# Three paced lanes for a delta rule: one layer of a hybrid encoder on one Trainium2 core

## The chip, the core and the metric

The kernel runs on one core of a Trainium2 chip. The metric is the device time of one execution in microseconds. The engines named below are PE (TensorE: matrix multiply; PEld are its weight loads), DVE (VectorE), ACT (ScalarE), POOL (GpSimd) and SP (SyncE, which here issues all DMAs). Each engine takes its instructions in order, and instructions on different engines wait for each other through semaphores.

## The reference

One layer runs over 512 tokens of a prompt and 8 x 16 tokens of running streams, 640 tokens in all, in float32:

```python
z = x @ w_in          # q, k, v, forget, gate of branch A; q|k|v, decay, beta, gate of branch B; two merge gates
# branch A: attention with forget gates, 8 heads of 128
y_a = (o_a * silu(gate_a)) @ w_out_fox
# branch B: gated delta rule, 8 heads of 128
conv = silu(sum(xpad[:, i:i + n_tok] * gdn_conv_w[i] for i in range(4)))
q_b, k_b = l2_normalize(q_b) * GDN_SCALE, l2_normalize(k_b)
u, w = solve(amat, v * beta), solve(amat, k * beta * exp(gc))   # triangular, per chunk
v_new = u_n - w_n @ s                                          # chunk after chunk
o = q_n @ s + qk_n @ v_new
s = s * gl_n + kt_n.T @ v_new
y_b = (rms_norm(o_b) * silu(gate_b)) @ w_out_gdn
h = (sigmoid(m_a) * y_a + sigmoid(m_b) * y_b) @ w_out
x1 = layer_norm(ALPHA * x + h)
x_out = x1 + sigmoid(x1 @ w_pl_gate) * rms_norm(p @ w_pl_proj)
```

It also returns keys, values, the last rows before the convolution and the final state matrices.

## The kernel before

Every large product is computed with the features on the partitions and the 640 tokens along the free axis, cut into two halves of 320. One **column** is 128 output features: 16 k-steps, each of six matmuls of 320 tokens (`mm6`, lines 216 to 221), because each float32 operand is split into a high and a low part in a faster format (high x high, high x low, low x high). The weights come in halves of a column by DMA (`w_dma`, line 155); `w_piece` (lines 160 to 173) makes pieces of four k-steps out of them: ACT casts the high part (line 169), DVE subtracts it for the low part (line 170). `PIECES` such pieces may be ahead of PE.

The work that is not a column runs in **lanes**. A lane is a queue of Python generators that emit instructions and then yield. After each k-step `column` calls `tick`, and each lane whose wake time has come emits its next step; `yield n` means "not again before n ticks". So the order in which instructions stand in each engine's queue is fixed by hand, in ticks, when the program is built. `until(cond)` ticks without emitting columns until a condition holds; `par` runs several generators within one lane.

The program has three phases.

1. `phase_fox`: the columns of branch A with attention as side work, the first `FRONT` merge-gate columns (`mcol`), and at its end two columns for the per-layer embedding, whose sum of squares is gathered in `eacc`, a tile that is kept until the tail.
2. `phase_gdn`: for each of eight heads the columns q, k, v and gate, then `FILL` = 1 merge-gate column (after the last head six). That makes 80 ticks per head. Side work per head:
   - `conv_silu` (lines 593 to 619), lane `conv`: four taps of 664 elements on DVE (lines 601 and 605), tanh on ACT (line 610), and two DVE operations that write k, q or v.
   - `gdn` (from line 621), lane `work`: transposes and norms, the triangular matrices `lt` and `qk`, then the solve of the 32 x 32 diagonal blocks: `lt` goes to DRAM and comes back in another layout (`lanes`), 31 steps of two DVE operations (lines 727 and 729) follow, two in each tick, and the result goes through DRAM to `u0`.
   - `gdn_chunks`, lane `chunks`: `gdn_pro` builds the inverse of the blocks (line 843 transposes `u0` into `m0` on DVE, line 852 is the first matmul that reads it) and runs the four chunks of the prompt (state update at line 909); `gdn_dec` does the streams.
   - `gdn_out`, lane `ends`: normalisation, gate, and the store of the head's output. The gate tile `sg` stays on the chip from its column until then (two buffers).

   Waits in the Python loop keep buffers safe: `bdone >= h - 2` before a head's k/q tile, `gdone >= h - 2` before its gate tile, and an empty convolution lane after each column. After the eighth head's six merge-gate columns two more follow, in which the 16 head outputs are loaded back; the last of these loads waits for `gdone == 7`.
3. `tail`: output projections, merge, layer norm and the embedding gate. It reads `eacc` in `rstd`, and begins with the loads of the merge gates (line 1219); the first use is line 1239.

All phases hold their tiles in pools that follow each other in the same memory.

Of the kernel before, what the change touches and what calls it, by code (L numbers as in the profile page):

```python
# [9 lines left out]
F32 = mybir.dt.float32  # L10
# [35 lines left out]

class Kernel:
# [5 lines left out]
    PIECES = 6  # L53
    FRONT = 32 - 11 - 7
    FILL = 1
    LATE = 3

    def __init__(self, tc, ins, outs):
        self.tc, self.nc, self.i, self.o = tc, tc.nc, ins, outs
        self.lanes = []  # L60
        self.now = 0


    def lane(self):
        q = {"gens": deque(), "wake": 0}
        self.lanes.append(q)
        return q

    def tick(self):
        self.now += 1  # L70
        for q in self.lanes:
            if q["gens"] and q["wake"] <= self.now:
                self.step(q)

    def step(self, q):
        while q["gens"]:
            try:
                n = next(q["gens"][0])
                q["wake"] = self.now + (n or 1)
                return  # L80
            except StopIteration:
                q["gens"].popleft()

    def until(self, cond):

        while not cond():
            self.tick()

    def par(self, *gens):

        live = [[g, 0] for g in gens]
        t = 0
        while live:
            for e in list(live):
                if e[1] <= t:
                    try:
                        e[1] = t + (next(e[0]) or 1)
                    except StopIteration:
                        live.remove(e)
            if live:  # L100
                yield 1
                t += 1
# [490 lines left out]
    def conv_silu(self, strip, ct, dst):  # L593
# [7 lines left out]
        nc.vector.tensor_scalar(out=y[:, 0:CV], in0=strip[:, 0:CV], scalar1=tp[:, 4 * ct:4 * ct + 1], scalar2=None,  # L601
                                op0=ALU.mult)
        yield
        for i in range(1, 4):
            nc.vector.scalar_tensor_tensor(out=y[:, 0:CV], in0=strip[:, i:i + CV],  # L605
                                           scalar=tp[:, 4 * ct + i:4 * ct + i + 1], in1=y[:, 0:CV],
                                           op0=ALU.mult, op1=ALU.add)
            yield
        th = self.zt([P, SW], "cth")
        nc.scalar.activation(th[:, 0:CV], y[:, 0:CV], AF.Tanh)  # L610
        yield 2
        nc.vector.scalar_tensor_tensor(out=dst[:, 0:NPT], in0=th[:, 0:NPT], scalar=1.0, in1=y[:, 0:NPT],
                                       op0=ALU.add, op1=ALU.mult)

        def dv(x):
            return x[:, NPT + 3:SW].rearrange("p (b r) -> p b r", r=19)[:, :, 0:16]
        nc.vector.scalar_tensor_tensor(out=dst[:, NPT:T].rearrange("p (b r) -> p b r", r=16), in0=dv(th), scalar=1.0,
                                       in1=dv(y), op0=ALU.add, op1=ALU.mult)
        yield

    def gdn(self, h, kq, v, sg):
# [48 lines left out]
        cs = self.zt([P, 5, 5], "cs", 2)  # L670
# [20 lines left out]
        lt = self.zt([P, 5, P], "lt")  # L691
        qk = self.zt([P, 5, P], "qk", 2)
        for t0 in (0, 2, 4):
# [16 lines left out]
            yield (4 if t0 < 4 else 1)  # L710

        for a in range(4):
            sl = slice(32 * a, 32 * a + 32)
            nc.sync.dma_start(out=self.ld[:, a].rearrange("t j i -> j t i"), in_=lt[sl, :, sl])
        nc.vector.tensor_tensor(out=gr, in0=gr, in1=kq[:, 1, :], op=ALU.mult)
        qg = gr
        yield 5
        lanes = self.zt([80, 32, 32], "hl", 1, "lanes")
# [21 lines left out]
        self.chunks["gens"].append(self.gdn_chunks(h, kq, lt, qk, qg, kt, vr, cs, u0, sg))  # L740

    def gdn_chunks(self, h, kq, lt, qk, qg, kt, vr, cs, u0, sg):
# [14 lines left out]
        self.bdone = h  # L757
        self.ends["gens"].append(self.gdn_out(h, self.ob, cs, sg))

    def gdn_out(self, h, ob, cs, sg):  # L760

        nc = self.nc
        junk = self.zt([P, P], "junk")
# [75 lines left out]
    def gdn_pro(self, h, kq, lt, qk, qg, kt, vr, cs, u0):  # L839
# [47 lines left out]
        for t in range(4):  # L887
            tl = slice(t * P, (t + 1) * P)
            if s is None:
                rp = vr[:, t, :]  # L890
            else:
                pd = self.sps()
                nc.tensor.matmul(pd[:, 0:P], kq[:, 0, tl], s, start=True, stop=True)
                rp = self.zt([P, P], "sq", 4, "rp")
                nc.vector.scalar_tensor_tensor(out=rp, in0=pd[:, 0:P], scalar=self.negc[:, t, h:h + 1],
                                               in1=vr[:, t, :], op0=ALU.mult, op1=ALU.add)
                yield 2
# [24 lines left out]
    def run(self, ctx):  # L922
# [10 lines left out]
        self.xd = dr([80, 256], F32, name="xd")  # L933
        self.vd = dr([5, P, 1024], F32, name="vd")
# [7 lines left out]
        self.chunks = self.lane()  # L942
# [12 lines left out]
    def phase_fox(self, work):  # L955
# [113 lines left out]
        self.eacc = self.cst.tile([P, T], F32, name="eacc")  # L1069
# [3 lines left out]
        self.proj(1, op)  # L1073

# [10 lines left out]
    def phase_gdn(self, conv, work):  # L1085
# [33 lines left out]
        kq = self.zt([P, 2, T], "kq", 2)  # L1119
        tiles = [kq[:, 0, :], kq[:, 1, :]]  # L1120
        tiles += [self.zt([P, T], t, n, "ogr") for t, n in (("strip", 1), ("cy", 1), ("sg", 2), ("v", 1), ("dt", 1))]
# [88 lines left out]
    def tail(self):  # L1210
# [9 lines left out]
        re = self.eacc  # L1220
        load(0)
        for n in range(16):
            def each(s):
                if s == 1 and n < 15:
                    load(n + 1)
                if s == 1 and n == 1:
                    self.work["gens"].append(self.rstd(None, self.eacc, RMS_EPS, re))
# [297 lines left out]
```

## Time and profile before

| | us |
|---|---|
| median of 3 runs | 2391.9 |
| lowest and highest | 2386.94, 2393.71 |
| profiled execution | 2391.51 |
| its span, first to last instruction | 2389.7 |
| DMA moved | 280.96 MB, 118 GB/s on average |
| DMA issues of weight halves (`wr`) | 290 of 512 KB |

The profile lists per engine how long it was busy, who waited for whom, and instructions in order of time. A row of instructions reads: line, engine, operation, written tile <- read tiles, shape, count, then busy time in all and the mean duration of one in ns, then idle time before and what ended it. Matmuls overlap in the records, so a matmul's duration is longer than its distance to the next. "Granted clock" is the share of full speed at which PE was allowed to run.

### The profile page before, as it was taken

Reading aid. Unit: us, or ns where it says so; the run is one execution under the profiler, and the core shown is the slowest. Engines: PE = TensorE matmul, PEld = TensorE weight load, DVE = VectorE, ACT = ScalarE, POOL = GpSimd, SP = SyncE. Lnnn points to the kernel's source line nnn. Section 1 sums busy time; section 2 is a strip of 40 time slices with the busy share of each in tenths; the row PEclk is TensorE's granted clock in tenths of the full one; section 3 lists DMA queues with packets and bytes.
Section 4 is the critical chain, followed back from the end, with each engine's and each line's share of the span. In section 5 each row is a group of like instructions: output and inputs, shape, how many; then the busy total and the mean of one; then the engine's idle time right before and its main releaser. Section 6 shows DMA issues by size and latency. Waiting matters only on the chain.

```text
span 2389.7 us, 39829 instructions
## 1 busy us (share of the span) xinstructions
PE 2322.5 (97%) x16274; PEld 2230.4 (93%) x16274; DVE 1177.2 (49%) x2589; ACT 728.4 (30%) x1656; POOL 83.2 (3%) x230
## 2 busy tenths in 40 slices
PE   9999999999999999999899898999999999999999
PEld 8999889999999999889788897899999999999999
DVE  5211223443433547476575765754633353657565
ACT  4222222322333432423334334232411131234222
POOL 0000000000000001010110101100000000010000
PEclk9999999999999999999899998999999999999999
DMA  6323236444444522221222222223633322233331
GB/s 222 104 93 102 98 137 220 167 168 168 168 159 141 186 76 95 76 90 64 79 93 87 80 73 86 91 79 110 218 127 124 115 102 99 95 105 110 115 118 63
DMA packets 107431, 280.96 MB, mean 118 GB/s; under 512 B 21464, under 2 KB 28712, under 8 KB 107248
## 3 DMA queue, kind: packets, MB, share of 16 engines
q1 hardware_dynamic: 107248, 278.41, 34.2%
q8 instruction: 128, 2.10, 0.4%
q14 instruction: 55, 0.45, 0.1%
HBM read 237.70 MB, written 40.67 MB: 116 GB/s over the span
## 4 chain that ended last, share of the span: by engine, by line
PE 87%; DVE 8%; ACT 2%; issue 1%; DMA 1%; SPq 0%; ACTq 0%
PE g L220 37%; PE g L221 36%; PE g L261 4%; DVE sx L727 2%; DVE sx L729 2%; DMA wr<-in_w 1%; DVE wl L170 1%; PE o L261 1%; ACT wh L169 1%; PE s L513 1%; DVE cy L605 1%; PE o L564 1%; PE s L473 1%; PE s L829 1%; PE s L699 1%
## 5 line engine op out<-in xcount | busy, mean ns | idle before, releaser
L170 DVE TENSOR_TENSOR wl<-wr,wh 128x512 fp32r<-128x512 f32 x584 | 402.3, 691 | 787.9 <-ACT wh L169 782.3
L220 PE MATMUL g<-xh,wh 128*128 128x320 f32 (+1 forms) x2160 | 701.2, 325 | 0.9 <-ACT xh L194 0.9
L220 PE MATMUL g<-xl,wh 128*128 128x320 f32 (+1 forms) x2160 | 673.1, 312 | 0.6 <-DVE xl L195 0.6
L221 PE MATMUL g<-xh,wh 128*128 128x320 f32 x2160 | 672.6, 311 | 0.0
L221 PE MATMUL g<-xl,wh 128*128 128x320 f32 x2160 | 672.2, 311 | 0.0
L220 PE MATMUL g<-xh,wl 128*128 128x320 f32 (+1 forms) x2160 | 671.2, 311 | 0.0
L221 PE MATMUL g<-xh,wl 128*128 128x320 f32 x2160 | 670.8, 311 | 0.0
L169 ACT CAST wh<-wr 128x512 fp32r<-128x512 f32 x584 | 361.3, 621 | 883.4 <-PE g L221 772.7
L220 PEld LDWEIGHTS g<-xh,wh 128*128 128x128 f32 x2160 | 411.0, 190 | 19.2 <-issue 14.2
L220 PEld LDWEIGHTS g<-xl,wh 128*128 128x128 f32 x2160 | 411.1, 190 | 1.2 <-DVE xl L195 1.1
L221 PEld LDWEIGHTS g<-xh,wh 128*128 128x128 f32 x2160 | 411.4, 190 | 0.8
L221 PEld LDWEIGHTS g<-xl,wh 128*128 128x128 f32 x2160 | 411.1, 190 | 0.0
L220 PEld LDWEIGHTS g<-xh,wl 128*128 128x128 f32 x2160 | 409.9, 190 | 0.3 <-DVE wl L170 0.3
L221 PEld LDWEIGHTS g<-xh,wl 128*128 128x128 f32 x2160 | 409.7, 190 | 0.0
L729 DVE TENSOR_TENSOR sx<-sx,sx 80x240 f32<-80x240 f32 (+14 forms) x240 | 68.3, 285 | 8.2
L727 DVE TENSOR_TENSOR sx<-sx,lanes 80x240 f32<-80x240 f32 (+14 forms) x240 | 68.3, 284 | 6.5
L605 DVE SCALAR_TENSOR_TENSOR cy<-strip,taps,cy 128x664 f32<-128x664 f32 x72 | 65.0, 902 | 1.6
L1239 DVE SCALAR_TENSOR_TENSOR sab<-sab,g 128x320 f32<-128x320 f32 x64 | 28.4, 485 | 69.0 <-PE g L220 64.1
L610 ACT ACTIVATE cth<-cy 128x664 f32<-128x664 f32 x24 | 18.2, 759 | 106.9 <-DVE cy L605 106.8
L261 PE MATMUL g<-wl,xh 128*128 128x512 f32 x128 | 50.6, 395 | 0.0
L261 PE MATMUL g<-wh,xl 128*128 128x512 f32 x128 | 50.4, 394 | 0.0
L261 PE MATMUL g<-wh,xh 128*128 128x512 f32 x128 | 50.4, 393 | 0.0
(338 smaller groups left out, 1879.2 us busy)
## 6 DMA issues: line engine op xcount, KB each, us to landing
wr<-in_w SPq DMA_DIRECT2D x290, 512.0 KB
kc<-in_kc SPq DMA_DIRECT2D x32, 512.0 KB
vc<-in_vc SPq DMA_DIRECT2D x32, 512.0 KB
xr<-in_xT SPq DMA_DIRECT2D x32, 320.0 KB
md<-m SPq DMA_DIRECT2D x32, 320.0 KB
sab<-md SPq DMA_DIRECT2D x32, 320.0 KB
ed<-e SPq DMA_DIRECT2D x16, 320.0 KB
el<-ed SPq DMA_DIRECT2D x16, 320.0 KB
```

The costliest lines, as they stand in the source:

```text
L169: nc.scalar.copy(out=hi, in_=src)
L170: nc.vector.tensor_tensor(out=lo, in0=src, in1=hi.bitcast(F32), op=ALU.subtract)
L220: nc.tensor.matmul(ps[0], whl[w], xhl[o][:, a], start=(first and x == 0), stop=(last and x == 2))
L221: nc.tensor.matmul(ps[1], whl[w], xhl[o][:, b], start=(first and x == 0), stop=(last and x == 2))
L261: nc.tensor.matmul(ps, x[:, sl], w, start=(s == 0 and n == 0), stop=(s == 15 and n == 2))
L473: nc.tensor.matmul(s1[32 * j:32 * j + 32, :], self.qpad[:, 2 * j + par, :], kc[:, (j % 2) * NPT:(j % 2 + 1) * NPT], start=(par == 0), stop ...
L513: nc.tensor.matmul(od[32 * j:32 * j + 32, 0:P], self.ppad[:, c, 2 * j + par, :], vc[:, o:o + P], start=False, stop=(par == 1 and c == 3), ...
L564: nc.tensor.matmul(ops[:, i * P:w], vn[:, kb, :], pT[:, kb * P:(kb + 1) * P], start=(kb == 0), stop=(kb == i))
L605: nc.vector.scalar_tensor_tensor(out=y[:, 0:CV], in0=strip[:, i:i + CV], scalar=tp[:, 4 * ct + i:4 * ct + i + 1], in1=y[:, 0:CV], op0=ALU. ...
L727: nc.vector.tensor_tensor(out=tmp[:, :, 0:n], in0=xo[:, :, j:j + 1].to_broadcast([80, 8, n]), in1=lanes[:, j:j + 1, j + 1:32].to_broadcast ...
L729: nc.vector.tensor_tensor(out=x[:, :, j + 1:32], in0=xo[:, :, j + 1:32], in1=tmp[:, :, 0:n], op=ALU.subtract)
L1239: nc.vector.scalar_tensor_tensor(out=x[:, sl], in0=x[:, sl], scalar=1.0, in1=ps[hf], op0=ALU.add, op1=ALU.mult)
```

## The change

- A `Meter` around DVE, ACT and PE sees each instruction as it is emitted and keeps a modelled clock: PE's time goes on with each matmul, DVE and ACT have an end time (`busy`) to which each instruction adds a cost by its number of elements. In `phase_gdn` (`paced`) a lane's next step needs, besides its ticks, that PE's clock has passed the end of the DVE and ACT instructions that the last step emitted, plus 0.25 us; with a negative yield, minus 1.5 us.
- The solve leaves `gdn` for a generator of its own, `gdn_blocks`, in a new lane `blocks`; with `chunks` three heads can be in work. `lt` gets a second and `cs` a third buffer, `lanes` a tile of its own (it shared one with the split operands), k/q two fixed tiles.
- The wait on `bdone` goes. The convolution of k waits in its lane until the head two before has issued the last read of its k tile (`kdone`), and the loop over columns waits only until the taps of the last convolution are emitted (`untapped`).
- The first of the four taps is multiplied on ACT instead of DVE.
- The gate tile is stored to DRAM (`sgd`) after its column and loaded again in `gdn_out`; `eacc` is stored to DRAM (`sqd`) at the end of `phase_fox` and loaded at the beginning of the tail, before the loads of the merge gates.
- `PIECES` goes from 6 to 5. `FRONT` goes from 14 to 12, and eight instead of six merge-gate columns follow the last head.

The core of the diff:

```diff
+class Meter:
+    def __init__(self, eng, seen):
+        self._eng, self._seen = eng, seen
+    def __getattr__(self, name):
+        f = getattr(self._eng, name)
+        if not callable(f):
+            return f
+        def call(*a, **k):
+            out = k.get("out", a[0] if a else None)
+            self._seen(name, out, a, k)
+            return f(*a, **k)
...
+        self.vector = Meter(nc.vector, kernel.saw_dve)
+        self.scalar = Meter(nc.scalar, kernel.saw_act)
+        self.tensor = Meter(nc.tensor, kernel.saw_pe)
...
-    PIECES = 6
-    FRONT = 32 - 11 - 7
+    PIECES = 5
+    FRONT = 32 - 13 - 7
     FILL = 1
+    FREE = 0.5
...
+    def saw(self, e, cost):
+        self.busy[e] = max(self.busy[e], self.clock) + cost
+    def saw_dve(self, name, out, a, k):
+        self.saw(0, 0.17 + 0.0011 * _free(out))
+    def saw_act(self, name, out, a, k):
+        if name != "dma_start":
+            self.saw(1, 0.21 + 0.00085 * _free(out))
+    def saw_pe(self, name, out, a, k):
+        rhs = a[2] if len(a) > 2 else k.get("rhs", a[1])
+        n, share = _free(out), out.shape[0] / P
+        full = (n + 32) / 2400.0 if rhs.dtype == F32R else 4 * n / 2400.0
+        self.clock += full * share
+    def watch(self, gen):
+        b = list(self.busy)
+        n = next(gen) or 1
+        if n == self.FREE or not self.paced:
+            return max(1, abs(n)), 0.0
+        t = max([y for x, y in zip(b, self.busy) if x != y] + [0.0])
+        return abs(n), t + (0.25 if n > 0 else -1.5)
...
     def tick(self):
         self.now += 1
         for q in self.lanes:
-            if q["gens"] and q["wake"] <= self.now:
+            if q["gens"] and q["wake"] <= self.now and q["t"] <= self.clock:
                 self.step(q)
     def step(self, q):
         while q["gens"]:
             try:
-                n = next(q["gens"][0])
-                q["wake"] = self.now + (n or 1)
+                n, q["t"] = self.watch(q["gens"][0])
+                q["wake"] = self.now + n
                 return
             except StopIteration:
                 q["gens"].popleft()
...
+            self.clock += 0.88
             self.tick()
...
-        live = [[g, 0] for g in gens]
+        live = [[g, 0, 0.0] for g in gens]
         t = 0
         while live:
             for e in list(live):
-                if e[1] <= t:
+                if e[1] <= t and e[2] <= self.clock:
                     try:
-                        e[1] = t + (next(e[0]) or 1)
+                        n, e[2] = self.watch(e[0])
+                        e[1] = t + n
                     except StopIteration:
                         live.remove(e)
             if live:
-                yield 1
+                yield self.FREE
                 t += 1
...
-        nc.vector.tensor_scalar(out=y[:, 0:CV], in0=strip[:, 0:CV], scalar1=tp[:, 4 * ct:4 * ct + 1], scalar2=None,
-                                op0=ALU.mult)
-        yield
+        nc.scalar.mul(y[:, 0:CV], strip[:, 0:CV], tp[:, 4 * ct:4 * ct + 1])
+        yield -1
         for i in range(1, 4):
             nc.vector.scalar_tensor_tensor(out=y[:, 0:CV], in0=strip[:, i:i + CV],
                                            scalar=tp[:, 4 * ct + i:4 * ct + i + 1], in1=y[:, 0:CV],
                                            op0=ALU.mult, op1=ALU.add)
-            yield
+            yield -1
...
+        self.untapped -= 1
         th = self.zt([P, SW], "cth")
         nc.scalar.activation(th[:, 0:CV], y[:, 0:CV], AF.Tanh)
         yield 2
+        while self.kdone < h - 2:
+            yield
...
-        cs = self.zt([P, 5, 5], "cs", 2)
+        cs = self.zt([P, 5, 5], "cs", 3)
...
-        lt = self.zt([P, 5, P], "lt")
+        lt = self.zt([P, 5, P], "lt", 2)
...
+        nc.vector.tensor_tensor(out=gr, in0=gr, in1=kq[:, 1, :], op=ALU.mult)
+        self.blocks["gens"].append(self.gdn_blocks(h, kq, lt, qk, gr, kt, vr, cs))
+    def gdn_blocks(self, h, kq, lt, qk, qg, kt, vr, cs):
+        nc = self.nc
         for a in range(4):
             sl = slice(32 * a, 32 * a + 32)
             nc.sync.dma_start(out=self.ld[:, a].rearrange("t j i -> j t i"), in_=lt[sl, :, sl])
-        nc.vector.tensor_tensor(out=gr, in0=gr, in1=kq[:, 1, :], op=ALU.mult)
-        qg = gr
...
-        lanes = self.zt([80, 32, 32], "hl", 1, "lanes")
+        lanes = self.zt([80, 32, 32], "lanes")
...
-        self.bdone = h
-        self.ends["gens"].append(self.gdn_out(h, self.ob, cs, sg))
-    def gdn_out(self, h, ob, cs, sg):
-        nc = self.nc
+        self.ends["gens"].append(self.gdn_out(h, self.ob, cs))
+    def gdn_out(self, h, ob, cs):
+        nc = self.nc
+        sg = self.zt([P, T], "og")
+        nc.sync.dma_start(out=sg, in_=self.sgd[h])
...
+                if t == 3:
+                    self.kdone = h
...
+        self.sqd = dr([P, T], F32, name="sqd")
+        self.sgd = [dr([P, T], F32, name=f"sgd{i}") for i in range(H)]
...
+        self.blocks, self.chunks = self.lane(), self.lane()
...
-        self.eacc = self.cst.tile([P, T], F32, name="eacc")
+        self.eacc = self.zt([P, T], "eacc")
...
+        nc.sync.dma_start(out=self.sqd, in_=self.eacc)
...
-        self.gdone = self.bdone = -1
+        self.kqs = [self.zt([P, 2, T], f"kq{i}") for i in range(2)]
+        self.gdone = self.kdone = -1
+        self.untapped = 0
+        self.paced = True
         for h in range(H):
             for c in range(4):
                 acc = self.column()[0]
-                if c == 0:
-                    self.until(lambda: self.bdone >= h - 2)
-                    kq = self.zt([P, 2, T], "kq", 2)
+                kq = self.kqs[h % 2]
                 if c == 2:
                     v = self.zt([P, T], "v")
-                self.until(lambda: not conv["gens"])
+                self.until(lambda: self.untapped == 0)
                 if c == 3:
-                    self.until(lambda: self.gdone >= h - 2)
-                    sg = self.zt([P, T], "sg", 2)
+                    sg = self.zt([P, T], "sg")
                     self.silu_evac(acc, sg, "cth")
+                    nc.sync.dma_start(out=self.sgd[h], in_=sg)
                 else:
                     ct = 8 * c + h
+                    self.untapped += 1
                     stp = self.strip_evac(acc, ct)
-                    conv["gens"].append(self.conv_silu(stp, ct, v if c == 2 else kq[:, 1 - c, :]))
-            work["gens"].append(self.gdn(h, kq, v, sg))
-            for _ in range(self.FILL if h < 7 else 6):
+                    conv["gens"].append(self.conv_silu(stp, ct, h if c == 1 else 0, v if c == 2 else kq[:, 1 - c, :]))
+            work["gens"].append(self.gdn(h, kq, v))
+            for _ in range(self.FILL if h < 7 else 8):
                 self.mcol("cth")
+        self.paced = False
...
-        re = self.eacc
+        re = self.zt([P, T], "re")
+        nc.sync.dma_start(out=re, in_=self.sqd)
         load(0)
```

More of the change, by code (lines that the diff above doesn't have):

```diff
@@ L44, in bcast, with __init__, __getattr__, _free @@
     return bass.AP(row_ap.tensor, row_ap.offset, [[0, reps], [1, n]])
+class Meter:
[9 more added lines that the diff above has]
+            return f(*a, **k)
+        return call
+class Metered:
+    def __init__(self, nc, kernel):
+        self._nc = nc
+        self.vector = Meter(nc.vector, kernel.saw_dve)
+        self.scalar = Meter(nc.scalar, kernel.saw_act)
+        self.tensor = Meter(nc.tensor, kernel.saw_pe)
+    def __getattr__(self, name):
+        return getattr(self._nc, name)
+def _free(ap):
+    n = 1
+    for x in ap.shape[1:]:
+        n *= x
+    return n
 class Kernel:
-    PIECES = 6
-    FRONT = 32 - 11 - 7
+    PIECES = 5
+    FRONT = 32 - 13 - 7
     FILL = 1
+    FREE = 0.5
     LATE = 3
     def __init__(self, tc, ins, outs):
-        self.tc, self.nc, self.i, self.o = tc, tc.nc, ins, outs
+        self.clock, self.busy, self.paced = 0.0, [0.0, 0.0], False
+        self.tc, self.nc, self.i, self.o = tc, Metered(tc.nc, self), ins, outs
         self.lanes = []
         self.now = 0
+    def saw(self, e, cost):
[17 more added lines that the diff above has]
+        return abs(n), t + (0.25 if n > 0 else -1.5)
     def lane(self):
-        q = {"gens": deque(), "wake": 0}
+        q = {"gens": deque(), "wake": 0, "t": 0.0}
         self.lanes.append(q)
@@ L591, in strip_evac, with conv_silu @@
         return st
-    def conv_silu(self, strip, ct, dst):
+    def conv_silu(self, strip, ct, h, dst):
         nc, tp = self.nc, self.taps
@@ L619, in conv_silu, with gdn @@
         yield
-    def gdn(self, h, kq, v, sg):
+    def gdn(self, h, kq, v):
         nc, cb = self.nc, self.cb
@@ L739, in gdn, with gdn_chunks @@
         yield 8
-        self.chunks["gens"].append(self.gdn_chunks(h, kq, lt, qk, qg, kt, vr, cs, u0, sg))
-    def gdn_chunks(self, h, kq, lt, qk, qg, kt, vr, cs, u0, sg):
+        self.chunks["gens"].append(self.gdn_chunks(h, kq, lt, qk, qg, kt, vr, cs, u0))
+    def gdn_chunks(self, h, kq, lt, qk, qg, kt, vr, cs, u0):
         nc, uu = self.nc, self.uu
@@ L941, in run @@
         work, conv, self.ends = self.lane(), self.lane(), self.lane()
-        self.chunks = self.lane()
+        self.blocks, self.chunks = self.lane(), self.lane()
         self.work = work
@@ L1098, in phase_gdn @@
                 acc = self.column()[0]
-                if c == 0:
-                    self.until(lambda: self.bdone >= h - 2)
-                    kq = self.zt([P, 2, T], "kq", 2)
+                kq = self.kqs[h % 2]
                 if c == 2:
                     v = self.zt([P, T], "v")
-                self.until(lambda: not conv["gens"])
+                self.until(lambda: self.untapped == 0)
                 if c == 3:
-                    self.until(lambda: self.gdone >= h - 2)
-                    sg = self.zt([P, T], "sg", 2)
+                    sg = self.zt([P, T], "sg")
                     self.silu_evac(acc, sg, "cth")
+                    nc.sync.dma_start(out=self.sgd[h], in_=sg)
                 else:
                     ct = 8 * c + h
+                    self.untapped += 1
                     stp = self.strip_evac(acc, ct)
-                    conv["gens"].append(self.conv_silu(stp, ct, v if c == 2 else kq[:, 1 - c, :]))
-            work["gens"].append(self.gdn(h, kq, v, sg))
-            for _ in range(self.FILL if h < 7 else 6):
+                    conv["gens"].append(self.conv_silu(stp, ct, h if c == 1 else 0, v if c == 2 else kq[:, 1 - c, :]))
+            work["gens"].append(self.gdn(h, kq, v))
+            for _ in range(self.FILL if h < 7 else 8):
                 self.mcol("cth")
+        self.paced = False
         nc.sync.dma_start(out=self.o["conv"], in_=self.tails)
         raw, nop = {}, [None] * KT
-        kq = self.zt([P, 2, T], "kq", 2)
+        kq = self.kqs[0]
         tiles = [kq[:, 0, :], kq[:, 1, :]]
-        tiles += [self.zt([P, T], t, n, "ogr") for t, n in (("strip", 1), ("cy", 1), ("sg", 2), ("v", 1), ("dt", 1))]
+        tiles += [self.zt([P, T], t, n, "ogr") for t, n in (("strip", 1), ("cy", 1), ("sg", 1), ("v", 1), ("dt", 1))]
         def load(k):
@@ L1226, in each @@
                 if s == 1 and n == 1:
-                    self.work["gens"].append(self.rstd(None, self.eacc, RMS_EPS, re))
+                    self.work["gens"].append(self.rstd(None, re, RMS_EPS, re))
             def after(s):
```

## The prediction, made before the result

> **What bounds the kernel now.** I read the page first, then the waits of PE, then busy time in three stretches.
>
> ```profile
> span 2389.7 us, 39829 instructions
> PE 2322.5 (97%) x16274; PEld 2230.4 (93%) x16274; DVE 1177.2 (49%) x2589; ACT 728.4 (30%) x1656; POOL 83.2 (3%) x230
> ```
> ```profile
> 0.00:920.00 920.00, 917.25 (x6387) 856.07 (x6388) 336.90 (x645) 275.85 (x594) 12.01 (x46) 1.00 0.43 147
> ```
> ```profile
> 920.00:1590.00 670.00, 610.81 (x4436) 584.82 (x4435) 425.53 (x1214) 231.56 (x684) 56.21 (x145) 0.94 0.24 80
> ```
> ```profile
> 1590.00:2389.70 799.70, 794.42 (x5455) 789.47 (x5453) 414.78 (x731) 220.96 (x379) 15.01 (x39) 1.00 0.34 115
> ```
> After the colon pair come the stretch's length, busy PE, PEld, DVE, ACT and POOL, then the granted clock, DMA share and GB/s. PE is the bound: 97% busy. What it loses lies in one place: idle 2.8 us before 920, 5.3 us after 1590, but 59.2 us in between, and only there is the clock below 1.00. That stretch is the delta-rule phase. Its waits on PE:
>
> ```profile
> PE s L852 <- DVE m L843: 34.0, 7, 5.2
> PE s L686 <- DVE S L909: 22.6, 7, 3.2
> PE s L904 <- ACT vn L901: 2.5, 7, 0.4
> ```
> 34.0 + 22.6 + 2.5 = 59.1 us: three waits per head, seven heads, and that is all of the idle time. The timelines of PE and DVE show what they are (start, duration, engine; in brackets the idle time before and its releaser).
>
> ```profile
> 1047.93 0.64 PE L852 MATMUL s<-m,lt 32*32 32x32 f32 x16 [4.89 <-DVE m L843]
> ...
> 1146.98 0.64 PE L852 MATMUL s<-m,lt 32*32 32x32 f32 x16 [4.84 <-DVE m L843]
> ```
> ```profile
> 983.42 0.65 PE L686 MATMUL s<-cb,v 128*128 128x128 f32 x4 [3.23 <-DVE S L909]
> ```
> ```profile
> 947.44 1.28 DVE L170 TENSOR_TENSOR wl<-wr,wh 128x512 fp32r<-128x512 f32 x2
> 948.89 0.75 DVE L170 TENSOR_TENSOR wl<-wr,wh 128x512 fp32r<-128x512 f32 x1 [0.16 <-ACT wh L169]
> 949.56 0.55 DVE L601 TENSOR_SCALAR cy<-strip,taps 128x664 f32<-128x664 f32 x1
> 950.04 0.30 DVE L843 STREAM_TRANSPOSE m<-u 128x128 f32<-128x128 f32 x1
> ```
> ```profile
> 979.47 0.68 DVE L664 TENSOR_TENSOR hl<-kq,hl 128x512 fp32r<-128x512 f32 x1
> ...
> 983.03 0.34 DVE L909 SCALAR_TENSOR_TENSOR S<-S,gl,s 128x128 f32<-128x128 f32 x1
> ```
> In both, a DVE operation of 0.3 us stands behind a queue of others: the transpose L843 behind weight splits and convolution, the state update L909 behind the 3.6 us from 979.47, in which the norms' small operations run. The lane's next step, due a fixed two ticks later, has meanwhile put its matmul into PE's order, and PE, which takes instructions in order, stops with all column work behind it. DVE as a whole is not full (425.53 of 670 us): the fault is when things are issued.
>
> Each long wait costs a second time. Six matmuls of one k-step, before and after the wait that ended at 950.39:
>
> ```profile
> 939.55 0.31 PE L220 MATMUL g<-xh,wh 128*128 128x320 f32 x1
> ...
> 940.43 0.31 PE L220 MATMUL g<-xh,wh 128*128 128x320 f32 x1
> ...
> 951.27 0.47 PE L221 MATMUL g<-xh,wh 128*128 128x320 f32 x1
> ...
> 952.87 0.47 PE L221 MATMUL g<-xh,wh 128*128 128x320 f32 x1
> ```
> ```profile
> 985.20:987.90 2.70, 2.70 (x12) 0.50 0.08 18
> ```
> A step takes 0.88 us before and 1.60 after, and the granted clock after the second kind of wait is 0.50 for at least 2.7 us. So 0.72 of each 1.60 us is lost, 1.2 us in 2.7; with the ends of the slow spell I take 1.4 us. With 14 long waits that is 20 us. Ends: 14 x 1.2 = 17 us, and 6% of 670 us = 40 us, the clock missing over the whole stretch, part of which fell in the waits themselves.
> The Trainium skill, "TensorE: Matmul & The Clock Gate", Part 1, says that PE drops to half clock after an idle window of about 3.4 us. The trace agrees on the half, but here a wait of 3.23 us is enough.
>
> **The change, part by part.**
> *Pacing* (the model clock) removes or adds no operation. In the delta-rule phase a lane's next step is now issued when the modelled clock of PE has passed the modelled end of that step's last DVE or ACT operation plus 0.25 us, with all that is queued there counted. So L843's consumer and L686 would be issued only when the DVE queue is through, and column matmuls take the place of the wait. All 59.1 + 20 = 79 us are open to it; no other stage is paced. How true is the model? For 664 elements the formula in the diff gives DVE 0.90 us, for 512 elements 0.73, for ACT's 664 elements 0.77, for a k-step 0.88:
>
> ```profile
> L605 DVE SCALAR_TENSOR_TENSOR cy<-strip,taps,cy 128x664 f32<-128x664 f32 x72 | 65.0, 902 | 1.6
> L170 DVE TENSOR_TENSOR wl<-wr,wh 128x512 fp32r<-128x512 f32 x584 | 402.3, 691 | 787.9 <-ACT wh L169 782.3
> L610 ACT ACTIVATE cth<-cy 128x664 f32<-128x664 f32 x24 | 18.2, 759 | 106.9 <-DVE cy L605 106.8
> L601 DVE TENSOR_SCALAR cy<-strip,taps 128x664 f32<-128x664 f32 x24 | 13.4, 557 | 0.0
> L727 DVE TENSOR_TENSOR sx<-sx,lanes 80x240 f32<-80x240 f32 (+14 forms) x240 | 68.3, 284 | 6.5
> ```
> It errs little and to the safe side on DVE. It does not see one engine waiting for another, DMA landings or POOL.
> *Three lanes.* The solve with its four DMA steps leaves the work lane for a lane of its own, so that preparation, solve and chunks belong to three heads. It is needed because pacing stretches the steps: the solve is 62 operations of 0.284 us, 17.6 us, issued before in 16 ticks of 0.88 = 14 us; now every step waits for its own end, 0.25 us and the next tick (0.44 on average), 17.6 + 16 x 0.69 = 29 us alone, some 40 with the other DVE work between. Counting yields the same way, preparation takes about 36 ticks, the solve lane 61 to 71, the chunks 31 up to the point that opens the new gate in the convolution (`kdone`): 128 to 138 ticks after a head's fourth column. The gate begins to hold up columns only when the convolution of v has to be through, two heads later: 58 + 2 x 80 - 64 = 154 ticks. So no cost, with 16 to 26 ticks in hand; each lane is under the 80 ticks of a head. If that cover is gone, each tick over is 0.88 us of idle PE in each of six heads.
> *First tap on ACT.* DVE gives 24 x 0.557 = 13.4 us, ACT takes 24 x 0.759 = 18.2 us (an operation of its kind, L610). Neither is PE's path by itself. But the second tap stands at the head of DVE's queue until ACT is through, and the -1 and -1.5 in the pacing let it be issued early. Ends: nothing, and one wait of 0.76 us for PE in each of the 21 convolutions that overlap other heads, 16 us. I take 6, nearer the lower end, since few matmuls wait for an operation just behind a tap.
> The Trainium skill, "ScalarE: Activation LUTs", Rules for kernel authors, says that a multiply belongs on VectorE and not on ScalarE. Here 557 against 759 ns agree; by that rule this part is a loss of 0.2 us per convolution, 24 x 0.2 = 5 us, if it reached PE.
> *Five weight pieces instead of six* shorten the lead of the splits from 6 x 4 x 0.88 = 21.1 to 17.6 us. The cover:
>
> ```profile
> ACT wh L169 <- PE g L221: 772.7, 337, 5.4
> ```
> The casts wait for PE to free a buffer, not PE for the casts, and the longest DVE backlog seen by PE is 5.2 us. Cost nothing; gone only with a backlog over 17 us.
> *Two merge-gate columns* move from the front to the end of the phase: no work more or less. They give the last head's chain (36 + 61 + 38 + 12 = 147 ticks) 8 x 16 + 24 = 152 ticks before the output load needs it. Unpaced it had 120. If the chain overran, each tick would be 0.88 us of idle PE, once.
> *Gate and sum of squares through DRAM* add 8 stores and 8 loads and one of each, 320 KB. All are SP's. The gate's store waits on SP for the last silu operation (under 1 us after issue), with weight loads behind it that are a lead of 17 us and more ahead; its load runs 14 ticks before use. The sum's load is put before the first two loads of the tail:
>
> ```profile
> 1706.07 1.75 SPq L1219 DMA_DIRECT2D sab<-md  x4
> ```
> ```profile
> 1708.85 0.89 DVE L1239 SCALAR_TENSOR_TENSOR sab<-sab,g 128x320 f32<-128x320 f32 x2 [4.86 <-DMA sab<-md]
> ```
> Its issue takes 1.75 / 4 = 0.44 us. DVE waits there already, but PE has two more PSUM buffers, a group of 8 x 0.88 = 7 us, to fill: nothing; without that cover up to the 2.8 us from issue to use.
> *Rest:* the second `lt`, third `cs`, own tile for the solve's `lanes` and fixed k/q tiles only allow the overlap.
>
> **Sum.** The profiled execution took 2391.5 us, 1.8 more than its span and 0.4 under the median of the runs, 2391.9. 2391.5 - 59.1 - 20 = 2312.4. Added: 6 for the tap, and the third kind of wait (2.5 us, ACT behind PE, which the model does not see): 8. **2320 us.** Bounds of this case: no residue and a clock loss of 30 gives 2302; residue 16 + 2.5 and a clock loss of 17 gives 2334.
> As a check by head: 1146.98 - 1047.93 = 99.1 us, of which five columns of 16 x 0.88 are 70.4; the forecast takes about 10 of the 28.7 others.
>
> **Rivals.**
> *A: shorter waits stay.* The model misses cross-engine waits (kt on ACT behind cs on DVE, PSUM buffers shared by three lanes), and half the idle time stays in pieces below 3 us. The clock then holds (0.4 us waits leave it at 1.00 in this row):
>
> ```profile
> 978.70:980.00 1.30, 1.30 (x12) 1.00 0.00 0
> ```
> Time: 2391.5 - 30 - 20 = 2342. For it: two of three waits ended on DVE in different steps, so others may come late next. Against: most steps have at least 1.76 us and the model counts the queue.
> *B: nothing gained.* The queue on DVE is work; what one matmul no longer waits for, another does. Time about 2390. Against: DVE has room.
>
> ```profile
> 1047.90:1147.00 99.10, 90.63 (x653) 86.88 (x653) 62.43 (x179) 34.25 (x102) 8.21 (x23) 0.93 0.25 82
> ```
> Of 62.4 us per head 1.7 leave; in a head of 88 us DVE would be 69% busy.
> *C: slower.* Paced lanes too long: preparation plus solve plus chunks exceed the 154 ticks, the gate in the convolution lane stays shut, and the loop that waits for the taps spins while no column is issued. It decides from 16 to 26 ticks (14 to 23 us) over my count; break-even is 79 / 6 = 13 us more in each of six heads. At 20 us per head it is 2391.5 - 79 + 120 = 2432. For it: my count has margins of a tenth. Against: it would need a quarter more.
>
> **How the numbers follow.** Forecast 0.65, A 0.21, B 0.05, C 0.09. A measurement can tell about 0.3%, 7.2 us. Faster: forecast, A and a little of B, 0.87; same 0.04; slower 0.09. The range takes the forecast's bounds and reaches over A: 2303 to 2352.
>
> **What would show it.** PE's waits of the delta-rule phase fall from 59 us to under 10, L852 and L686 no longer lead them; the granted clock there is 1.00; a head takes about 88 us; DVE's busy time falls by 13 us, ACT's rises by 18. Waits of 3 us and more left on PE, or a last chain through DMA at the phase's end, would make it wrong.

## The result, and the profile after

The changed kernel takes 2306.9 us (median of 4 runs, 2305.7 to 2307.5) against 2389.4 us for the kernel before, run beside it (4 runs): a ratio of 0.9654, 95% interval 0.9633 to 0.9675, 3.5% faster. The forecast was 2320 us, with 2303 to 2352 as its range.

The head of the page of the changed kernel, then busy time in three stretches (the middle one is again the delta-rule phase; columns as in the prediction: busy PE, PEld, DVE, ACT, POOL, granted clock, DMA share, GB/s):

```profile
span 2305.7 us, 39849 instructions
## 1 busy us (share of the span) xinstructions
PE 2292.5 (99%) x16274; PEld 2205.0 (96%) x16274; DVE 1160.2 (50%) x2565; ACT 748.0 (32%) x1680; POOL 67.2 (3%) x230
```
```profile
0.00:892.00 892.00, 888.54 (x6184) 826.72 (x6185) 327.09 (x630) 271.29 (x585) 11.75 (x46) 1.00 0.44 148
892.00:1545.00 653.00, 648.42 (x4906) 627.72 (x4905) 448.83 (x1304) 266.57 (x748) 42.09 (x151) 1.00 0.31 102
1545.00:2305.70 760.70, 755.52 (x5188) 750.58 (x5186) 384.23 (x632) 210.16 (x349) 13.33 (x33) 1.00 0.35 117
```
PE does the same 16274 matmuls. In the delta-rule phase it is idle 4.6 us where it was idle 59.2, and the clock there is 1.00 where it was 0.94. DVE lost 17 us of work and ACT gained 20. The 24 first taps are 13.4 us of DVE's (measured in e5) and 20.9 us of ACT's, 871 ns each, where the forecast had 759 ns and 18.2 us.

All of PE's waits in the changed kernel (all its instructions carry line 61, that of the `Meter`, so they are told apart by their tiles):

```profile
PE s L61 <- ACT junk L61: 2.2, 3, 1.3
PE s L61 <- DVE og L61: 2.1, 1, 2.1
PE s L61 <- DMA kc<-in_kc: 1.4, 1, 1.4
PE wu L61 <- DVE z L61: 1.2, 1, 1.2
PE g L61 <- DVE xl L61: 0.5, 2, 0.3
PE g L61 <- ACT xh L61: 0.2, 1, 0.2
```
The two long waits, on `m` (34.0 us) and `S` (22.6 us), and the short one on `vn` (2.5 us) are no longer there. The first two rows are what is left of the phase, 4.3 us. The heads on the timeline, by the first matmul that reads `m`, in the changed kernel and then in the kernel before:

```profile
953.46 0.44 PE L61 MATMUL s<-m,lt 32*32 32x32 f32 x16
...
1548.83 0.44 PE L61 MATMUL s<-m,lt 32*32 32x32 f32 x16
```
```profile
950.39 0.52 PE L852 MATMUL s<-m,lt 32*32 32x32 f32 x16 [4.52 <-DVE m L843]
...
1633.61 0.44 PE L852 MATMUL s<-m,lt 32*32 32x32 f32 x16
```
In the changed kernel it starts with no idle time before it, and from the first head's to the last's it is 1548.83 - 953.46 = 595.4 us, 85.1 for each of seven heads. Before it was 683.2 us, 97.6 each (99.1 is one of them; 88 was forecast). The lanes also moved against the columns, so this is a rough measure of what a head costs.

Where the 84.0 us between the two spans (2389.7, 2305.7) came from can be read off. Listed waits of PE sum to 61.8 us before and 7.6 after: 54.2 us. The other 29.8 us are what PE's same matmuls took less, which is the low clock; for 14 long waits that is 2.1 us each on average. The section on why the prediction was right reads it from the clock itself.

### The profile page after: what moved, and what is told of

Read it like the earlier page. It is cut to its first block, busy times and chain, and to the rows that moved or that the text cites. A ratio compares the mean times of both kernels' runs of the same rounds, so it can differ in the third digit from the quotient of the medians.

```text
span 2305.7 us, 39849 instructions
## 1 busy us (share of the span) xinstructions
PE 2292.5 (99%) x16274; PEld 2205.0 (96%) x16274; DVE 1160.2 (50%) x2565; ACT 748.0 (32%) x1680; POOL 67.2 (3%) x230
## 5 line engine op out<-in xcount | busy, mean ns | idle before, releaser
L61 PE MATMUL g<-xh,wh 128*128 128x320 f32 (+2 forms) x4352 | 1024.9, 316 | 0.2 <-ACT xh L61 0.2
L61 PE MATMUL g<-xl,wh 128*128 128x320 f32 (+2 forms) x4352 | 997.4, 309 | 0.5 <-DVE xl L61 0.5
L61 PE MATMUL g<-xh,wl 128*128 128x320 f32 (+2 forms) x4352 | 995.2, 309 | 0.0
L61 PEld LDWEIGHTS g<-xh,wh 128*128 128x128 f32 x4352 | 719.9, 189 | 19.1 <-issue 13.6
L61 PEld LDWEIGHTS g<-xl,wh 128*128 128x128 f32 x4352 | 731.2, 189 | 1.0 <-DVE xl L61 1.0
L61 PEld LDWEIGHTS g<-xh,wl 128*128 128x128 f32 x4352 | 730.8, 188 | 0.2
L61 ACT ACTIVATE m<-g 128x320 f32<-128x320 f32 x64 | 24.9, 448 | 53.5 <-PE g L61 49.1
L61 ACT COPY strip<-g 128x320 f32<-128x320 f32 (+2 forms) x72 | 19.7, 348 | 34.9 <-PE g L61 34.9
L61 PEld LDWEIGHTS g<-wh,xl 128*128 128x128 f32 x128 | 24.0, 188 | 5.7
L61 PEld LDWEIGHTS g<-wh,xh 128*128 128x128 f32 x128 | 24.0, 188 | 5.7
```

The source lines that it names most:

```text
L61: return f(*a, **k)
```

## The experiments

Each was run beside the kernel before on the same chip, but not all of them on one chip, so ratios are compared. "Waits" is the sum of PE's listed waits in the profile, "clock" the mean granted clock of the profiled run. The changed kernel is in the first row.

| run | us | ratio to before (95%) | waits, us | clock |
|---|---|---|---|---|
| the change | 2306.9 | 0.9654 (0.9633 to 0.9675) | 7.6 | 0.999 |
| e1 no pacing | 2405.0 | 1.0063 (1.0042 to 1.0085) | 72.8 | 0.986 |
| e2 pacing alone | 2377.9 | 0.9950 (0.9937 to 0.9963) | 42.3 | 0.981 |
| e3 six columns at the end | 2317.3 | 0.9698 (0.9676 to 0.9720) | 15.0 | 0.999 |
| e4 issue 1.75 us earlier | 2336.1 | 0.9778 (0.9756 to 0.9801) | 28.2 | 0.993 |
| e5 first tap on DVE | 2310.3 | 0.9666 (0.9653 to 0.9679) | 10.7 | 1.000 |
| e6 longer solve lane | 2334.7 | 0.9762 (0.9744 to 0.9780) | 24.4 | 0.994 |
| e7 accumulators in the model | 2306.2 | 0.9646 (0.9633 to 0.9659) | 6.3 | 1.000 |
| e8 four weight pieces | 2306.0 | 0.9648 (0.9635 to 0.9661) | 7.6 | 0.999 |
| e9 before, two yields | 2379.5 | 0.9953 (0.9939 to 0.9966) | 59.8 | 0.986 |
| e10 e6, output lane first | 2332.1 | 0.9754 (0.9740 to 0.9767) | 24.9 | 0.994 |
| e11 e7, output lane first | 2301.6 | 0.9629 (0.9616 to 0.9642) | 4.2 | 1.000 |
| e12 before, three yields | 2328.8 | 0.9755 (0.9734 to 0.9776) | 26.2 | 0.999 |

My theory was that the time came from *when* a lane's next step is issued. The rival was that the new lanes, the buffers and the lighter DVE took the collisions away.

### e1: the change without its clock

```diff
-        self.paced = True
+        self.paced = False
```

> The changed kernel with the model clock never consulted (paced stays False): three lanes, buffers, the first tap on ACT, DRAM detours and column counts stay. Theory 1, the time came from issuing a lane's next step only when DVE's queue is through: the waits of PE on DVE come back, about 59 us of them in the delta-rule phase, and with them the low clock (0.98 over the span); the time is 2307 + 54 + 28 = 2389 us, 2370 to 2400. Theory 2, the lanes of their own and the tap taken from DVE removed the collisions: the time stays below 2330 us and PE waits under 20 us in all.

2405.0 us, 0.6% slower than before. PE's waits in this run:

```profile
PE s L61 <- DVE m L61: 34.6, 8, 5.1
PE s L61 <- DVE S L61: 22.4, 7, 3.2
PE s L61 <- ACT vn L61: 12.2, 7, 2.0
```
The two old waits are back (34.0 and 22.6 us before), and the third has grown from 2.5 to 12.2 us. Whether the taps on ACT did that is not shown: in e12, with the taps on DVE, it grew too, to 7.9. So without the pacing nothing of the gain is left: lanes, buffers, tap and DRAM detours alone cost 14 us. The rival falls.

### e2: the clock without the rest

The kernel before with `Meter`, `watch` and the paced `tick` and `par` of the change, `paced` set over the loop of heads, and nothing else.

> The kernel before with the model clock alone: preparation, solve and output of the solve stay in one lane, the old waits on bdone, gdone and the empty convolution lane stay, first tap on DVE, six weight pieces. Counting ticks in this order, the one lane needs more than a head's 80 and the loops over columns tick about 172 times without a column. Theory 1 with the lane budget: the old waits go (minus 83 us), but 172 x 0.88 = 151 us of idle PE come instead, and some 10 us of low clock behind them: 2389 - 83 + 151 + 10 = 2467 us, 2430 to 2490. Theory 2 would have it that pacing is not what matters: 2389 within 10 us. If pacing alone were enough: 2310 to 2330.

2377.9 us: 13 us better than before, 89 us under my figure. So pacing in one lane gives 13 of the 83 us, and this pacing needs what the change adds to it, as forecast. (That a gain needs three lanes does not follow: e12 has most of it in the old lanes.) But the price I put on a tick without a column, 0.88 us of idle PE, is wrong. The 172 ticks are there when the program is built, and all of PE's listed waits are 42.3 us, not 151. Such a tick puts nothing into PE's queue. PE goes straight on with the column that is emitted later; it waits only where the lane's own matmuls stand in those ticks. There it does. Two stretches between columns of one head, then the part of the second in which the clock is low (columns as above):

```profile
1160.00:1180.00 20.00, 18.77 (x182) 16.77 (x180) 8.11 (x31) 11.30 (x39) 1.23 (x3) 0.91 0.19 64
1180.00:1200.00 20.00, 16.58 (x87) 14.44 (x87) 9.49 (x29) 4.51 (x16) 0.05 (x1) 0.74 0.12 40
1189.53:1203.18 13.65, 11.98 (x46) 11.00 (x47) 6.43 (x16) 4.70 (x19) 0.38 (x2) 0.50 0.16 42
```
In the second row PE is busy 83% of the time and no wait is over 1.6 us, and the clock is at 0.74. That is a mean of two clocks: full speed up to 1189.5 us, then half speed for 13.7 us, in the first 9 of which PE has only small matmuls of the chunks and the preparation, with short waits between them. So PE can be slowed without any long wait. That such sparse work is the cause is my reading; no run separates it.

### e3: the last head's cover taken away

```diff
-    FRONT = 32 - 13 - 7
+    FRONT = 32 - 11 - 7
...
-            for _ in range(self.FILL if h < 7 else 8):
+            for _ in range(self.FILL if h < 7 else 6):
```

> The changed kernel with the two merge-gate columns back at the front (FRONT 14, six columns behind the last head). By my count of ticks the last head's chain then lacks 22 ticks of columns. If those ticks are idle PE: 22 x 0.88 = 19 us and about 2 us of low clock, 2307 + 21 = 2328 us, in one stretch at the end of the phase. If the chain's own length is hidden by the two columns behind it anyway: 2307 us.

2317.3 us: 10 us, half of the 21 expected. 22 ticks are missing, but PE waits only where it meets the chain's own matmuls, most of all the output's transposes:

```profile
1604.75 0.49 PE L61 MATMUL s<-vn,kt 128*128 128x128 f32 x2 [1.12 <-ACT vn L61]
1614.51 1.65 PE L61 MATMUL s<-cb,ob 128*128 128x128 f32 x5 [5.84 <-ACT ob L61]
```
The two columns behind the last head are worth those 10 us; the other reading, that the chain is hidden anyway, falls.

### e4: what a wait costs

```diff
-        return abs(n), t + (0.25 if n > 0 else -1.5)
+        return abs(n), t + (-1.5 if n > 0 else -1.5)
```

> The changed kernel with the margin of all paced steps at -1.5 us in place of +0.25, so that a step may be issued up to 1.75 us too soon; else unchanged. Tells what short waits cost. If a wait costs its own length and a wait below 2 us leaves the clock alone: many waits of at most 2 us, 10 to 40 us in all, granted clock 0.995 or more, time 2307 plus those waits. If any wait of PE costs the clock as the long ones of the kernel before did (1.4 to 2 us each): a granted clock of 0.98 and a time that rises by about twice the waits.

2336.1 us, and not many waits but one in each of seven heads, 2.5 to 5.7 us long:

```profile
PE s L61 <- DVE m L61: 24.5, 7, 5.7
```
One of them, DVE first, then ACT, then PE:

```profile
1041.42 0.69 DVE L61 TENSOR_TENSOR wl<-wr,wh 128x512 fp32r<-128x512 f32 x1 [0.86 <-ACT wh L61]
1042.03 0.30 DVE L61 STREAM_TRANSPOSE m<-u 128x128 f32<-128x128 f32 x1
```
```profile
1037.68 1.40 ACT L61 ACTIVATE kt<-s,cs 128x128 f32<-128x128 f32 x5 [3.39 <-DVE cs L61]
...
1040.71 0.68 ACT L61 CAST wh<-wr 128x512 fp32r<-128x512 f32 x1
```
```profile
1042.48 0.64 PE L61 MATMUL s<-m,lt 32*32 32x32 f32 x16 [3.12 <-DVE m L61]
```
DVE had nothing to do, but its queue was held by a weight split (`wl`) that waited for ACT's cast, which stood behind `kt` and `vr`, and `kt` had waited 3.39 us for DVE's `cs`. That is a wait from engine to engine that the model does not count; with +0.25 us the same step starts without a wait. In the spans, 27.9 us more with 20.6 us more of waits: 1.0 us on top for each of seven waits, and a clock of 0.993. So neither of my two cases: waits of this length cost the clock, but less than the 2.1 us of the kernel before. A margin above +0.25 was not tried.

### e5, e7, e8: tap, accumulators, pieces

```diff
 # e5
-        nc.scalar.mul(y[:, 0:CV], strip[:, 0:CV], tp[:, 4 * ct:4 * ct + 1])
+        self.saw_act('mul', y[:, 0:CV], (), {})
+        nc._nc.vector.tensor_scalar(out=y[:, 0:CV], in0=strip[:, 0:CV], scalar1=tp[:, 4 * ct:4 * ct + 1],
+                                    scalar2=None, op0=ALU.mult)
 # e7
-            self.saw(1, 0.21 + 0.00085 * _free(out))
+            self.saw(1, (0.30 if 'accum_out' in k else 0.21) + 0.00085 * _free(out))
 # e8
-    PIECES = 5
+    PIECES = 4
```

> The changed kernel with the first tap back on DVE (tensor_scalar) while the model still books it on ACT, so that every other instruction stands where it stood. Theory of the prediction: the tap on ACT costs PE up to 6 us, since the second tap waits at the head of DVE's queue: 2301 us, waits of PE on ACT and DVE in the delta phase gone from 4 us. Rival: with pacing nothing on PE hangs on it, 2307 within 4 us, DVE's busy time up by 13 us and ACT's down by 18. Third: DVE, fuller by 0.56 us per convolution than the model knows, makes new waits: 2310 or more.

> The changed kernel with a truer model: ACT operations that also accumulate are booked 0.09 us longer (the traces show 0.40 us from one to the next where the model has 0.32). It is the version that might be better than both: the three waits on the squares (ACT junk, 2.2 us) go, the one of 2.1 us on DVE may move. 2303 to 2307 us. If waits only move from one step to another: 2307 us and as many us of waits.

> The changed kernel with four weight pieces ahead of PE in place of five. Theory of the prediction: the lead of 4 x 4 x 0.88 = 14 us is still far over any backlog on DVE: 2307 within 4 us. Rival: the lead is short where side work is dense (moments in the tail, convolution and solve in the delta phase), and the sixth piece that the change gave up was not free: waits of PE on the split weights (wl) appear, 2315 us or more.

The tap (e5), on DVE in e5 and on ACT in the changed kernel:

```profile
L673 DVE TENSOR_SCALAR cy<-strip,taps 128x664 f32<-128x664 f32 x24 | 13.4, 558 | 0.0
```
```profile
L61 ACT ACTIVATE cy<-strip,taps 128x664 f32<-128x664 f32 x24 | 20.9, 871 | 0.4 <-DVE kq L61 0.4
```
2310.3 us, 3 us more, its interval overlapping that of the change. PE has 3.1 us more of waits, 1.2 of them new and on DVE's `S`. Both the second case (within 4 us) and the third (2310 or more) allow that time; the first falls: the tap on ACT costs nothing here, and whether it gains a little is not settled. The Trainium skill's rule ("ScalarE: Activation LUTs", Rules for kernel authors) that a multiply belongs on VectorE is right about the operation (558 against 871 ns) and decides nothing about this kernel's time. Accumulators (e7): no difference; the one wait on `og` went, but those on `junk` grew from 2.2 to 3.8 us. The wait moved, as the second case had it. Pieces (e8): 2306.0 us, no difference, though the lead is cut again. No wait on `wl` appears, and 1.2 us on `wh`. The fifth piece is free, so the sixth, one step further from the need, can be taken to have been free too.

### e6 and e10: a lane that is longer, within its slack

```diff
 # e6, at the end of gdn_blocks
-        yield 8
+        yield 18
 # e10, in addition
-        work, conv, self.ends = self.lane(), self.lane(), self.lane()
+        self.ends, work, conv = self.lane(), self.lane(), self.lane()
```

> The changed kernel with ten more ticks between the end of the solve and the chunks (a yield of 18 in place of 8), in every head. By count of ticks the gate in the convolution then opens 143 to 154 ticks after a head's fourth column, within the 154, and the last head's chain ends 3 ticks before it is needed. If slack is what the count says, nothing: 2307 within 4 us. If the length of the lanes sets the pace, ten ticks in each of seven heads: 7 x 10 x 0.88 = 62 us, 2369 us.

2334.7 us: 28 us more, where my count of slack said nothing and the other case 62. PE's waits name the cause:

```profile
PE s L61 <- DVE og L61: 20.0, 6, 3.8
```
PE and DVE around one of them:

```profile
1114.07 0.71 PE L61 MATMUL s<-cb,ob 128*128 128x128 f32 x5
1120.94 1.11 PE L61 MATMUL s<-cb,v 128*128 128x128 f32 x4 [3.51 <-DVE og L61]
```
```profile
1116.28 0.68 DVE L61 TENSOR_TENSOR hl<-kq,hl 128x512 fp32r<-128x512 f32 x1
...
1120.08 0.16 DVE L61 TENSOR_SCALAR cs<-rry 128x5 f32<-128x5 f32 x1
1120.15 1.00 DVE L61 SCALAR_TENSOR_TENSOR og<-s,cvec,og 128x512 f32<-128x512 f32 x2
```
The output lane of one head has its transposes done at 1114.8, but the two operations that read them stand behind the 3.9 us of norms of another head's preparation. The next transposes of that preparation (`cb,v`) need the PSUM buffer, and PE waits. The model lets a step wait for its own operations, not for another lane's that hold a buffer. In the changed kernel the same thing happens once, 2.1 us; ten ticks more bring the two lanes into step in six heads. So it is not the length of the lane but what it meets.

> The run with ten more ticks in the solve lane, with one more edit: the lane that writes a head's output is served ahead of the preparation in each tick. Theory: the 24 us of the run before came from one collision, the output's two DVE operations issued in the same tick behind the norms of the preparation, with PE waiting for the PSUM buffer that they free; with the order turned they stand ahead of the norms, the six waits of 3.4 us and the low clock go, 2307 to 2311 us. Rival: the longer lane costs by its length: 2330 us or more as before.

2332.1 us, and six waits on `og` as before (19.6 us). Serving the output lane first did not put its operations ahead of the norms, so this run did not test the cure that I had in mind. That the wait is on `og` behind the norms is shown by the rows; that turning their order would give back the 28 us stays open.

### e9 and e12: the same by hand

Is a model needed, or only the late issue? Two numbers in the kernel before, then a third:

```diff
 # e9 and e12: gdn_pro, after the transpose of u0; gdn, before the transposes of v
-        yield 2
+        yield 8
-        yield 2
+        yield 6
 # e12 alone: gdn_dec, before the first product with st
-        yield 6
+        yield 15
```

> The kernel before with two numbers changed and nothing else: the wait after the transpose of u0 (line 843) 8 ticks in place of 2, the one before the transposes of v (line 686) 6 in place of 2. Theory: what counts is that these two steps are issued late enough, not that a model says when. Then the two waits (34.0 + 22.6 us) and the low clock behind them go, and the time comes near the changed kernel's, 2310 to 2325 us. Rival: later chunks meet other work, and waits of the same kind come elsewhere (in the chunk steps behind convolution or norms); then 2340 to 2390 us, and only pacing of all steps gets the whole gain.

2379.5 us, in the rival's range. Both old waits are gone, and a new one has their place:

```profile
PE s L801 <- DMA st<-in_st: 46.7, 8, 7.7
```
SP and PE in one head of this run, then SP and the chain of work at the same place in the kernel before:

```profile
1047.00 0.43 SPq L746 DMA_DIRECT2D st<-in_st  x1
```
```profile
1053.28 1.08 PE L801 MATMUL s<-st,kpad 128*32 128x128 f32 x16 [6.84 <-DMA st<-in_st]
```
```profile
1046.09 0.42 SPq L746 DMA_DIRECT2D st<-in_st  x1
```
```profile
1055.52 0.57 PE s L801 x16
```
Before, the state's load was issued at 1046.09, while PE stood until 1047.93 for `m`, and PE came to this product at 1055.52, 9 us after the issue. The old wait had covered the load; without it PE is there before the load is issued.

> The kernel before with three numbers changed: the two of the run before (8 and 6 ticks), and the streams' first product waits 15 ticks in place of 6 after the head's state is asked for, since without the old wait PE came to it up to 7.7 us before the state had landed. Theory: three late issues are the whole of the loss; the 46.7 us on the load and the low clock behind them go, 2379 - 47 - 11 = 2321 us, 2312 to 2328. Rival: again another step comes late (the streams' later steps now beside the prompt's), 2335 us or more: then the model clock's worth is that it moves all steps at once.

2328.8 us, just above the 2312 to 2328 that were expected: 62 of the 83 us, with three numbers and the lanes of the kernel before. What is left in this run:

```profile
PE s L852 <- DVE m L843: 12.4, 6, 2.1
PE s L904 <- ACT vn L901: 7.9, 7, 1.1
PE s L899 <- DVE rp L895: 2.9, 7, 0.4
```
```profile
core 0: 2326.2 us, clock 0.999
```
```profile
1312.08:1315.49 3.41, 3.41 (x35) 3.02 (x34) 1.90 (x5) 0.63 (x3) 0.50 (x1) 0.50 0.57 198
```
These waits are all at most 2.1 us, and the clock holds almost everywhere: only behind one of the six waits of 2.1 us is it at half, for 3.4 us (last row). The span is 20.5 us over the changed kernel's with 18.6 us more of waits: here short waits cost little more than their own length. That is about the price that rival A of the prediction gave them.

### e11: a version that may be better

e7 with the lane order of e10.

> The changed kernel with the output lane served first and the accumulating ACT operations booked 0.09 us longer: meant to take the last waits of the delta-rule phase (2.1 us on DVE og, 2.2 us on ACT junk). 2302 to 2306 us if they go; 2307 us if the waits move.

2301.6 us. The wait on `junk` is gone and 0.7 us is left of that on `og`:

```profile
PE s L61 <- DVE og L61: 0.7, 1, 0.7
```
Its single times (2300.7 to 2304.5) lie under all those of the change (2305.7 to 2307.5), but they are from another chip and the intervals of the ratios touch. Clearly better than the kernel before; 5 us better than the change is likely and not settled.

## Why the prediction was right

- **The bound and the mechanism.** PE in order, held by matmuls issued before a DVE queue is through: shown by e1 (all waits back) and e12 (gone by late issue alone).
- **The idle time.** 59.1 us open to the change; 4.3 are left in the phase. The residue of 8 us was too high, and it had the wrong parts: the 6 us for the tap are not there (e5), although the operation took 871 ns and not 759, and the 2.5 us on `vn` went. The 4.3 us are on `junk` and `og`, which the sum did not have. That 8 and 4.3 are of one size is luck.
- **The clock.** Taken at 20 us, 1.4 for each long wait, with ends of 17 and 40; measured 29.8 us, 2.1 each. This is the term of the sum that was most mis-sized. The profile's granted clock shows how: the phase before the change has 13 spells at half clock, three of 3.4 us and ten of 6.8, 78.5 us together. Below are the first spell, a long one with the time behind it, and 8.4 us from the start of the one long wait (3.2 us) that had no spell; the clock is the third figure from the end:

```profile
950.60:954.01 3.41, 3.41 (x28) 3.34 (x20) 3.07 (x4) 2.25 (x6) 3.20 (x4) 0.50 0.87 320
1145.16:1151.99 6.83, 5.01 (x53) 4.55 (x53) 5.19 (x9) 2.77 (x7) 5.26 (x10) 0.50 0.66 230
1152.00:1155.00 3.00, 3.00 (x36) 2.58 (x36) 1.46 (x4) 0.37 (x1) 0.00 (x0) 1.00 0.00 0
1276.56:1285.00 8.44, 5.21 (x39) 5.21 (x40) 3.78 (x20) 3.74 (x13) 0.00 (x0) 1.00 0.09 19
```
Half of 78.5 us is lost, 39.3; 8.6 of that falls into the long waits, where it costs nothing; 30.6 remain, and the changed kernel still has one spell, 1.7 us. That leaves 28.9 of the 29.8 us. The prediction read its 1.4 us off the first head, whose two spells are both among the short ones, and used the mean clock of the phase (6% of 670 us) only for the upper end. Small matmuls run slowly in a spell too: the four transposes of `v` that the prediction quotes with 0.65 us come just before theirs, and in four of the seven heads they took 1.11 us. The two terms, 9.8 and 3.7 us, less 0.6 us of waits elsewhere and the rounding of the forecast, make the 12.5 us by which the saving (71.5 forecast, 84.0 in the spans) was short. Both misses went the same way, so the time came out near the low end of the range.
- **The rivals.** C needed lanes longer than 154 ticks. The program's own count gives 32 to 34 ticks for preparation, 62 to 74 for the solve and a gate that opens 132 to 143 ticks after the fourth column; forecast 36, 61 to 71 and 128 to 138. The last head's chain ends 10 ticks before it is needed (5 forecast). So C did not decide. But its price was wrong: a tick without a column is not 0.88 us (e2, e3). A is real as a mechanism: e4 and e6 show the engine-to-engine wait and the shared PSUM buffer that it named, worth 29 and 28 us when the lanes fall badly. In the change as it stands they happen to cost 4.3: both kinds of wait that are left are for a PSUM buffer that another lane's operations still read.
- **"Slack costs nothing"** held for the pieces (e8) and the two DRAM detours (no wait on them in the list), and failed for the lane (e6): the slack was there, and the time rose by a collision that a count of ticks does not show.

## What to carry to other kernels

On an engine that takes its work in order, ask of each small step not how long it takes but whether its input is ready when it is put in the queue. One instruction issued too soon stops everything behind it, so a late issue costs nothing as long as other work fills its place, and an early one costs its wait and, if that is long, mostly the clock after it too. Read what the clock costs as a sum over the whole phase, not off one spell. When a stall goes, list what used to be ready thanks to it (here a load), and expect that to be late next. A schedule that paces each lane by its own operations is still at the mercy of what two lanes share; change the length of one lane and look again.

## What the runs showed of the hardware that I had not expected

- PE's granted clock was 0.50 for 13.7 us in which PE was busy 88% of the time, with no wait over 1.6 us in it or in the 20 us before it (e2). The Trainium skill ("TensorE: Matmul & The Clock Gate", Part 1) ties the drop to an idle window of about 3.4 us; the same page also says that the gate follows how busy PE has been, and that reading fits this row better.
- The low clock came in spells of 3.4 or 6.8 us at half speed in the kernel before, and the length of a wait does not alone decide it: of seven waits of 3.2 us one had no spell, and one of six waits of 2.1 us had one (e12). The mean clock was 0.999 in e12, and 0.993 with seven waits of 2.5 to 5.7 us (e4).
- An ACT operation of 128 elements that also accumulates takes 0.40 us from one to the next: each is followed by an instruction of its own that reads the accumulator (0.2 us).
